# Plain float32 matmuls in place of three split float32r passes in the dense stages of a decoder layer

## The chip, the cores and the metric

The kernel runs on one core of a Trainium2 chip. The metric is the time of one execution in microseconds (us), measured on the device; lower is better.

## The reference

The reference computes one layer of a decoder trunk on 1,056 tokens (1,024 of a prompt, and 32 of eight sequences that are being decoded, four each), all in float32, with width 1,024. Cut to what matters:

```
h = rms_norm(x)
z = h @ w_in                         # u, v, q, six key/value parts, gates, merge gates
u = gelu(u); v = layer_norm(gelu(v)) # 512 wide each
o_a = u * (w_s @ v + b_s)            # causal mixing in chunks of 128 tokens
kc, vc = compress(keys), compress(values)          # dense product, gelu, dense product
o_b = g0*attend(q, kc, vc) + g1*attend(q, selected blocks) + g2*attend(q, window)
x = x + (sigmoid(g_a) * (o_a @ w_branch_a) + sigmoid(g_b) * (o_b @ w_branch_b)) @ w_out
y = x + square(relu(rms_norm(x) @ w_up)) @ w_down  # 4,096 wide
```

The caches of the decoded sequences (16 pages of 128 keys each) are compressed and attended as well.

## The kernel before

A matmul of this chip takes two forms on float32 data here. A *plain* one takes operands of type float32. One on *float32r* operands reads values that have been rounded to fewer bits of mantissa. To come near float32 accuracy with float32r, the kernel splits each operand `a` into a high part (the copy `cp` to float32r, on ScalarE) and a low part (`a - high`, on VectorE or GpSimd), and makes three passes: high times high, high times low, low times high, all adding up in one PSUM bank. Every dense product of a 128x128 stationary tile and up to 512 moving columns is three `matmul` calls.

The work in order:

- **Start and projections (0 to about 233 us).** X, scaled by the norm's gains, is kept transposed in SBUF as a high and a low tile for eight slices of 128 channels. The token-major projections (keys and values, then v, then q; `mm3`) take nine blocks of 128 tokens, each eight products of 512 columns, with weights `wt`, split ahead (`wt_split`). The feature-major parts kc, vc (`fm_k`, weights `wk`) and the gates take eight slices times three chunks of 352 tokens. The gating unit mixes v in between (`v_mix`).
- **Prompt attention (to about 741 us).** 32 pairs of 128-query block and head pair: logits, softmax, transposition of the weights P, product with the values. These matmuls are float32r already, or transposes, and aren't changed. In between run two other streams: the compression of the caches (`c_load`, `hl`), and "fillers", the dense blocks of merge gates and u that need neither attention (`fillers`, `Weights`). POOL scales P, and for those two streams it makes the low parts.
- **Attention of the decoded tokens (to about 901 us)**, which uses plain float32 matmuls before the change too: `s_acc` (logits, 512 columns; the code calls it 40 times in this stage with the ring of pages) and `values` (256 columns). The last fillers run beside it.
- **Dense tail (to the end).** Branch (16 half blocks of four slices), output projection (8 blocks of eight slices), and the MLP (64 blocks of eight slices), each slice times three chunks of 352 tokens (`fm_block`). Sources OA, OU, M, H and U are each a high and a low tile. OA and OU are read back from memory in pieces `ol` that are then split.

The weight blocks of fillers and tail come through the class `Weights`: load `wraw`, split into `whl`, one split and two loads ahead. For the fillers (`W0`) there is one buffer of each; for the tail (`W1`) two. The order of each engine's instructions is made ahead of time by the compiler's scheduler from priorities; the order of the SP queue is written by hand in the cache and page stages.

Of the kernel before, what the change touches and what calls it, by code (L numbers as in the profile page):

```python
# [45 lines left out]
def build(tc, a):  # L46
# [48 lines left out]
    class Weights:  # L95
        """The feature-major weight blocks ids, loaded and split ahead of their use."""

        def __init__(self, pl, n, ids):
            self.pl, self.n, self.ids = pl, n, list(ids)
            self.raw, self.hl, self.nl, self.ns = [], [], 0, 0  # L100
# [9 lines left out]
        def split(self):  # L110
            i = self.ids[self.ns]
            if self.nl <= self.ns:
                self.load()
            t = self.pl.tile([128, 2, 8, 128], F32R, name="whl", bufs=self.n)
            raw = self.raw.pop(0)
            with tc.high_priority():
                cp(t[:, 0], raw)
                (POOL if i < FM_BR else DVE).tensor_tensor(t[:, 1], raw, f(t[:, 0]), op=OP.subtract)  # L118
            self.hl.append(t)
            self.ns += 1  # L120

        def get(self, i):
            """Block i; its place in the order is checked."""
            if not self.hl:
                self.split()
            assert self.ids[self.ns - len(self.hl)] == i
            return self.hl.pop(0)

        def ahead(self):
            """One split and two loads past the blocks handed out."""  # L130
            used = self.ns - len(self.hl)
            while self.ns < min(used + 1, len(self.ids)):
                self.split()
            while self.nl < min(used + 2, len(self.ids)):
                self.load()
# [3 lines left out]
    ones = const("ones", [128, 128], dt=F32R)  # L139
# [8 lines left out]
    X = big.tile([128, 2, 8, NT], F32R, name="big1")  # L148
# [15 lines left out]
    DVE.memset(f(ones), 1.0)  # L164
    cp(expo, f(ones)[:, 0:16], scale=-0.5)

    # ---------------------------------------------------------------- phase 1
# [9 lines left out]
    wtr = {}  # L177

    def wt_load(g, k):
        wtr[g, k] = pr.tile([128, 512], F32, name="wtr", bufs=2)  # L180
        SP.dma_start(wtr[g, k], a["wtok"][g, k])

    def wt_split(g, k):
        t = p1.tile([128, 2, 512], F32R, name="wt", bufs=8)
        split(t[:, 0], t[:, 1], wtr.pop((g, k)))
        wt[g, k] = t

    wkr = {}

    def wk_load(i):  # L190
        wkr[i] = pw.tile([128, 8, 128], F32, name="wkr")
        SP.dma_start(wkr[i].rearrange("p k n -> p (k n)"), a["wfm"][i])

    def wk_split(i):
        t = pw.tile([128, 2, 8, 128], F32R, name="wk")
        split(t[:, 0], t[:, 1], wkr.pop(i))
        return t

    def mm3(out, xs, ws, k, first, last):
# [4 lines left out]
    def fm_k(pss, w, k, first, last, B=None):  # L204
        src = X if B is None else B
        for c in range(3):
            mm(pss[c][:, 0:TB], w[:, 0, k], src[:, 0, k, c * TB:(c + 1) * TB], first, False)
        for c in range(3):
            mm(pss[c][:, 0:TB], w[:, 0, k], src[:, 1, k, c * TB:(c + 1) * TB], False, False)
        for c in range(3):  # L210
            mm(pss[c][:, 0:TB], w[:, 1, k], src[:, 0, k, c * TB:(c + 1) * TB], False, last)
# [14 lines left out]
    wk_load(0)  # L226
# [10 lines left out]
    def x_split(k, cs):  # L237
        cp(X[:, 0, k, cs], xk[:, cs], scale=gvec[:, k:k + 1])
        DVE.scalar_tensor_tensor(X[:, 1, k, cs], xk[:, cs], gvec[:, k:k + 1], f(X[:, 0, k, cs]), op0=OP.mult, op1=OP.subtract)

    for k in range(8):
        xk = xr.pop(k)
        if k == 0:
            with tc.high_priority():
                x_split(k, slice(0, 512))
                wt_split(0, k)
                x_split(k, slice(512, NT))
            wkc = wk_split(0)
        else:
            x_split(k, slice(0, NT))  # L250
            wt_split(0, k)
# [11 lines left out]
        for n in range(NK0):  # L263
            mm3(tokps[n], slice(tok0(n), tok0(n) + 128), wt[0, k], k, k == 0, k == 7)
        fm_k(kcps, wkc, k, k == 0, k == 7)

    with tc.high_priority():
        add(accs[0], accs[0], accs[1])
        ah = [px.tile([128, NT], F32R, name="ah%d" % h, tag="xr", bufs=XRB) for h in range(2)]
        split(ah[0], ah[1], accs[0])  # L270
        pstv = pst[:, 0:18].rearrange("p (n c) -> p n c", c=2)
        for n in range(NB):
            xs = slice(tok0(n), tok0(n) + 128)
            for h in range(2):
                mm(pstv[:, n], ah[h][:, xs], ones[:, 0:2], h == 0, h == 1)
# [15 lines left out]
    wg_r = pv.tile([128, 8, 24], F32, name="wg_r")  # L291
    SP.dma_start(wg_r, a["wgate"])
    wg = pv.tile([128, 2, 8, 24], F32R, name="wg")
    for k in range(2):
# [14 lines left out]
    def head_rstd(z3, h, post):  # L309
        """z3 (128, h, 64) -> (128, h) of rsqrt(mean square + eps) * post."""  # L310
# [48 lines left out]
    def gates():  # L359
        """The attention gates, feature-major, then token-major through the tensor engine."""  # L360
        pss = [bank(*t) for t in fm3]
        for k in range(8):
            for i, j in ((0, 0), (0, 1), (1, 0)):
                for c in range(3):
                    mm(pss[c][0:24, 0:TB], wg[:, i, k], X[:, j, k, c * TB:(c + 1) * TB], k + i + j == 0, k == 7 and i == 1)
# [29 lines left out]
    def c_evac(which, pss, n0=0):  # L395
        """Raw kc / vc rows, feature-major, from their PSUM."""
# [40 lines left out]
    def comp_hidden(ps, nch, bias, pl):  # L437
        """ps (128, 2, nch): first | second halves; returns twice the gelu as (kv h, chunk)."""
# [18 lines left out]
    def comp_knorm(ps, pl, gkc, nb):  # L457
        """(chunk, (kv d)) PSUM -> normed rows in SBUF."""
# [13 lines left out]
    split(wg[:, 0], wg[:, 1], wg_r)  # L472
# [41 lines left out]
    for c in range(3):  # L514
# [7 lines left out]
        dh = pv.tile([128, 2, 384], F32R, name="dh", bufs=1)  # L522
        split(dh[:, 0, 0:w], dh[:, 1, 0:w], dg[:, 0:w])
        prb = bank("O", 1)
        for h in range(2):
            mm(prb[:, 0:w], ones, dh[:, h, 0:w], h == 0, h == 1)
        cp(rep[:, c * 384:c * 384 + w], prb[:, 0:w])
    c_evac(0, kcps)
    for n in range(NK0, NB):
        xs = slice(tok0(n), tok0(n) + 128)  # L530
        ps = bank("S", 3)
        for k in range(8):
            mm3(ps, xs, wt[0, k], k, k == 0, k == 7)
            if n == NB - 1:
                wt.pop((0, k))
                if k + 2 < 8:
                    wt_load(2, k + 2)
                wt_split(2, k)
# [4 lines left out]
    wk_load(1)  # L543
    w = wk_split(1)
# [21 lines left out]
    # the gating unit  # L566
# [12 lines left out]
    wsr = pg.tile([128, 8, 128], F32, name="wsr", tag="vh", bufs=2)  # L579
    SP.dma_start(wsr, a["wsT"])  # L580
    wsh = pg.tile([128, 2, 8, 128], F32R, name="wsh")
# [967 lines left out]
```

## Time and profile before

| | |
|---|---|
| median of three runs | 1854.61 us (1849.91 to 1858.01) |
| span of the profiled execution | 1851.7 us (nothing of its time outside the span is listed) |
| TensorE (PE) busy | 1796.6 us, 97% |
| VectorE (DVE), ScalarE (ACT), GpSimd (POOL) busy | 974.2, 718.1, 414.0 us |

PE is matmuls, PEld the loads of stationary tiles, which overlap them. A matmul's record runs from its start to its modelled end, and the next one starts before that end, so that the sum of durations, and "busy", say less than the distance from one start to the next.

### The profile page before, as it was taken

The page shows a single profiled execution, that of the slowest core. Times are in us where ns is not written, and L with a number is a line of the kernel's source. Part 1 is how long each engine was busy: PE and PEld are TensorE (multiplying, and loading weights), DVE is VectorE, ACT ScalarE, POOL GpSimd, SP SyncE. Part 2 cuts the span into 40 slices and gives each one's busy share as a digit, 9 for nine tenths or more (in the row PEclk, how much of TensorE's full clock was granted, in tenths as well). Part 3 has the DMA queues.
Part 4 walks back from the last instruction along what each step waited for, and adds up shares of the span by engine and source line. Part 5 has one row for each costly group of instructions (what it writes and reads, how often), then busy time and mean ns, then how long its engine had stood idle before and what let it go on. Part 6 is the DMA issues. An engine that isn't in the chain of part 4 may idle for free.

```text
span 1851.7 us, 30386 instructions
## 1 busy us (share of the span) xinstructions
PE 1796.6 (97%) x11031; PEld 1687.7 (91%) x11031; DVE 974.2 (53%) x2459; ACT 718.1 (39%) x1747; POOL 414.0 (22%) x604
## 2 busy tenths in 40 slices
PE   8999989999899999999899999999999999999999
PEld 6877889999899998666599999999999999999999
DVE  7637778777767777255465445333333333333332
ACT  5534577767667765233322332300330033003300
POOL 3103456555556655210000220000000000000000
PEclk9999989999999999999899999999999999999999
DMA  6232454333323314665453221111111111111121
GB/s 197 93 96 63 141 152 122 96 91 93 94 68 98 99 60 128 193 202 183 128 162 123 90 85 46 46 46 46 46 46 46 46 46 46 46 46 46 42 79 65
DMA packets 158264, 168.74 MB, mean 91 GB/s; under 512 B 52385, under 2 KB 132898, under 8 KB 158114
## 3 DMA queue, kind: packets, MB, share of 16 engines
q1 hardware_dynamic: 140466, 135.78, 23.5%
q0 software_dynamic: 6464, 20.19, 3.2%
q10 hardware_dynamic: 11184, 10.83, 1.8%
q8 instruction: 87, 1.43, 0.3%
q14 instruction: 63, 0.52, 0.1%
HBM read 136.56 MB, written 29.13 MB: 89 GB/s over the span
## 4 chain that ended last, share of the span: by engine, by line
PE 84%; DVE 6%; DMA 3%; ACT 3%; SPq 2%; issue 2%; POOL 2%; ACTq 0%; DVEq 0%; POOLq 0%
PE S L73 27%; PE G L73 17%; PE PT L73 14%; PE O L73 11%; PE F L73 11%; PE PT L844 2%; SPq L932 1%; DMA ol<-o_d 1%; ACT P L783 1%; DVE S L774 1%; DMA wraw<-wfm 1%; POOL hl L977 1%; POOL P L798 1%; DVE PH L57 1%; DMA xr<-xT 0%
## 5 line engine op out<-in xcount | busy, mean ns | idle before, releaser
L73 PE MATMUL G<-big,whl 128*128 128x352 f32 x1344 | 265.2, 338 | 2.9 <-DVE zt L57 1.5
L54 ACT ACTIVATE whl<-wraw 128x1024 fp32r<-128x1024 f32 x100 | 106.1, 1061 | 411.9 <-PE S L73 144.4
L73 PEld LDWEIGHTS G<-big,whl 128*128 128x128 f32 x1344 | 220.6, 192 | 17.6 <-issue 9.9
L73 PE MATMUL S<-U,whl 128*128 128x352 f32 x864 | 201.6, 324 | 0.0
L73 PE MATMUL S<-H,whl 128*128 128x352 f32 x840 | 190.4, 324 | 0.0
L73 PE MATMUL PT<-U,whl 128*128 128x352 f32 x576 | 154.9, 324 | 0.0
L73 PEld LDWEIGHTS S<-U,whl 128*128 128x128 f32 x864 | 150.0, 188 | 0.0
L798 POOL TENSOR_SCALAR P<-P,rs 128x128 f32<-128x128 f32 (+4 forms) x272 | 132.7, 502 | 62.3 <-DVE rs L57 40.9
L73 PEld LDWEIGHTS S<-H,whl 128*128 128x128 f32 x840 | 144.9, 188 | 0.0
L73 PE MATMUL PT<-H,whl 128*128 128x352 f32 x528 | 143.2, 324 | 0.0
L783 ACT ACTIVATE P<-S,nm 128x512 f32<-128x512 f32 (+3 forms) x208 | 108.9, 531 | 44.1 <-DVE nm L57 33.0
L73 PE MATMUL S<-wt,big 128*128 128x512 f32 x408 | 104.1, 402 | 11.4 <-ACT wt L54 7.9
L57 DVE TENSOR_TENSOR PH<-PT,PH 128x512 fp32r<-128x512 f32 (+2 forms) x160 | 98.1, 618 | 28.2 <-ACT PH L54 26.7
L118 DVE TENSOR_TENSOR whl<-wraw,whl 128x1024 fp32r<-128x1024 f32 x80 | 97.7, 1221 | 15.5 <-ACT whl L54 15.5
L73 PEld LDWEIGHTS PT<-U,whl 128*128 128x128 f32 x576 | 103.3, 188 | 0.0
L73 PEld LDWEIGHTS S<-wt,big 128*128 128x128 f32 x408 | 76.3, 191 | 28.4 <-ACT wt L54 7.9
L73 PE MATMUL F<-H,whl 128*128 128x352 f32 x312 | 101.1, 324 | 0.0
L73 PE MATMUL O<-PH,V 128*128 128x256 f32 x528 | 91.6, 295 | 8.3 <-DVE PH L57 7.9
L54 ACT ACTIVATE PH<-PT 128x512 fp32r<-128x512 f32 (+2 forms) x160 | 86.1, 544 | 34.9 <-PE PT L844 34.2
L73 PE MATMUL O<-H,whl 128*128 128x352 f32 x312 | 99.0, 324 | 0.0
L73 PE MATMUL S<-KT,QT 128*128 128x128 f32 (+3 forms) x416 | 96.2, 342 | 2.9 <-ACT P L783 2.1
L73 PE MATMUL G<-H,whl 128*128 128x352 f32 x312 | 97.5, 324 | 0.5 <-DVE r L1384 0.5
(375 smaller groups left out, 3935.5 us busy)
## 6 DMA issues: line engine op xcount, KB each, us to landing
wraw<-wfm SPq DMA_DIRECT2D x80, 512.0 KB, 3.3
ring<-cs SPq DMA_DIRECT2D x128, 128.0 KB, 2.1
wraw<-wfm POOLq DMA_DIRECT2D x20, 512.0 KB, 3.8
tg<-th_d SPq DMA_DIRECT2D x48, 176.0 KB, 2.9
qdl<-qd_d SPq DMA_DIRECT2D x64, 128.0 KB, 2.5
raw<-cck SPq DMA_DIRECT2D x128, 64.0 KB, 1.9
raw<-ccv SPq DMA_DIRECT2D x128, 64.0 KB, 1.8
wtr<-wtok SPq DMA_DIRECT2D x24, 256.0 KB, 2.6
```

Source lines behind the costliest of these rows:

```text
L54: return ACT.activation(out, in_, AF.Copy, scale=scale)
L57: return DVE.tensor_tensor(out, x, y, op=op)
L73: return PE.matmul(out, l, r, start=start, stop=stop, skip_group_check=skip)
L118: (POOL if i < FM_BR else DVE).tensor_tensor(t[:, 1], raw, f(t[:, 0]), op=OP.subtract)
L774: DVE.tensor_tensor_reduce(S, S, m, scale=-1.0, scalar=3e38, op0=OP.add, op1=OP.min, accum_out=dst)
L783: ACT.activation(Ps[c][:, lo:hi], Ss[c][:, lo:hi], AF.Exp, bias=nm[:, 0, k:k + 1], scale=todo[h, br, i], accum_out=sm[:, i, k:k + 1])
L798: POOL.tensor_scalar(P, P, rs[:, 1, k:k + 1], 1.0, op0=OP.mult, op1=OP.mult)
L844: PE.transpose(pt[:, j], Ps[c][:, j * 128:(j + 1) * 128], ident)
L932: SP.dma_start(dst, src)
L977: (POOL if qt else DVE).tensor_tensor(hl[:, 1], raw[:, :, cols], f(hl[:, 0]), op=OP.subtract)
```

## The change

All dense products, and the mixing, norm sums and cache compression, take plain float32 operands in one `matmul` call. The split tiles and their instructions go. Weights are used as loaded (`wfb`, four buffers in the tail and three for the fillers; `wt` with 16 buffers). X is one scaling on DVE. OA and OU are loaded straight into place, and M and U have two buffers.

```diff
-    X = big.tile([128, 2, 8, NT], F32R, name="big1")
+    X = big.tile([128, 8, NT], F32, name="big1")
...
     class Weights:
...
         def load(self):
-            t = self.pl.tile([128, 8, 128], F32, name="wraw", bufs=self.n)
+            t = self.pl.tile([128, 8, 128], F32, name="wfb", bufs=self.n)
...
-            t = self.pl.tile([128, 2, 8, 128], F32R, name="whl", bufs=self.n)
-                cp(t[:, 0], raw)
-                (POOL if i < FM_BR else DVE).tensor_tensor(t[:, 1], raw, f(t[:, 0]), op=OP.subtract)
...
         def ahead(self):
-            while self.ns < min(used + 1, len(self.ids)):
-                self.split()
-            while self.nl < min(used + 2, len(self.ids)):
+            while self.nl < len(self.ids) and len(self.raw) < self.n - 1:
                 self.load()
...
-        mm(out, X[:, 0, k, xs], ws[:, 0], first, False)
-        mm(out, X[:, 0, k, xs], ws[:, 1], False, False)
-        mm(out, X[:, 1, k, xs], ws[:, 0], False, last)
...
+            DVE.tensor_scalar(X[:, k, cs], xk[:, cs], gvec[:, k:k + 1], None, op0=OP.mult)
...
-            mm3(ps, xs, wt[0, k], k, k == 0, k == 7)
+            mm(ps, X[:, k, xs], wt[0, k], k == 0, k == 7)
...
-            for qt in range(4):
-                hl = pa.tile([128, 2, 16, 32], F32R, name="hl", bufs=HIB)
-                    cp(hl[:, 0], raw[:, :, cols])
-                    (POOL if qt else DVE).tensor_tensor(hl[:, 1], raw[:, :, cols], f(hl[:, 0]), op=OP.subtract)
...
-                    mm(out, w1[:, 0, qt * 2 + o], hv[:, o], qt + o == 0, False)
-                    mm(out, w1[:, 1, qt * 2 + o], hv[:, o], False, False)
-                    mm(out, w1[:, 0, qt * 2 + o], lv[:, o], False, qt == 3 and o == 1)
+            rv = raw.rearrange("p g (o k r) -> p o k g r", k=2, r=8)
+            for o in range(8):
+                mm(out, w1[:, o], rv[:, o], o == 0, o == 7)
...
-    W1 = Weights(wst, 2, range(FM_MG + NF0, N_FM))
+    W1 = Weights(wst, 4, range(FM_MG + NF0, N_FM))
...
-    W0 = Weights(wst0, 1, range(FM_MG, FM_MG + NF0))
+    W0 = Weights(wst0, 3, range(FM_MG, FM_MG + NF0))
...
-                t = olp.tile([128, TB], F32, name="ol", bufs=OLB)
-                ACT.dma_start(t[:, 0:e], o_d[4 * half + k, :, cs])
-                split(dst[:, 0, k, cs], dst[:, 1, k, cs], t[:, 0:e])
+            e = NP if half else NT
+            ACT.dma_start(dst[:, k, 0:e], o_d[4 * half + k, :, 0:e])
...
     def fm_block(w, src, ks, woff=0):
...
             for c in range(3):
-                mm(pss[c][:, 0:TB], w[:, 0, k + woff], src[:, 0, k, c * TB:(c + 1) * TB], first, False)
-            for c in range(3):
-                mm(pss[c][:, 0:TB], w[:, 0, k + woff], src[:, 1, k, c * TB:(c + 1) * TB], False, False)
-            for c in range(3):
-                mm(pss[c][:, 0:TB], w[:, 1, k + woff], src[:, 0, k, c * TB:(c + 1) * TB], False, last)
+                mm(pss[c][:, 0:TB], w[:, k + woff], src[:, k, c * TB:(c + 1) * TB], i == 0, i == len(ks) - 1)
...
-                DVE.scalar_tensor_tensor(r, pss[c][:, 0:TB], 0.0, r, op0=OP.max, op1=OP.mult)
-                cp(U[:, 0, fo, cs], r)
-                sub(U[:, 1, fo, cs], r, f(U[:, 0, fo, cs]))
+                DVE.scalar_tensor_tensor(U[:, fo, cs], pss[c][:, 0:TB], 0.0, r, op0=OP.max, op1=OP.mult)
```

## Rows read from the trace of the kernel before

**Rows 1.** The page: busy time of the engines, and PE in 40 equal slices.
```profile
PE 1796.6 (97%) x11031; PEld 1687.7 (91%) x11031; DVE 974.2 (53%) x2459; ACT 718.1 (39%) x1747; POOL 414.0 (22%) x604
...
PE   8999989999899999999899999999999999999999
```
**Rows 2.** Four stretches: length, busy time (instructions) by engine, granted clock, DMA share, GB/s.
```profile
0.00:233.00 233.00, 221.37 (x1144) 185.64 (x1145) 155.95 (x394) 112.69 (x215) 65.47 (x69) 1.00 0.37 117
233.00:741.00 508.00, 478.93 (x3396) 461.09 (x3394) 381.05 (x1213) 348.39 (x1014) 302.15 (x485) 0.98 0.34 100
741.00:901.00 160.00, 153.18 (x728) 101.83 (x728) 67.27 (x207) 51.08 (x150) 23.45 (x30) 0.99 0.58 180
901.00:1852.00 951.00, 943.08 (x5766) 939.18 (x5766) 369.96 (x648) 205.93 (x370) 22.94 (x21) 0.99 0.19 65
```
**Rows 3.** The chain that ended last: start us, us, what, and how many instructions.
```profile
130.25 11.42 PE S L73 x48
...
254.84 2.38 POOL whl L118
...
1263.57 11.68 PE S L73 x72
```
**Rows 4.** The stretches after 233 us, instructions on `whl` alone (columns as in Rows 2).
```profile
233.00:741.00 508.00, 211.50 (x1104) 180.97 (x1104) 0.00 (x0) 17.97 (x17) 38.94 (x17) 0.98 0.34 100
741.00:901.00 160.00, 73.88 (x337) 55.28 (x337) 2.45 (x2) 5.28 (x5) 9.39 (x4) 0.99 0.58 180
901.00:1852.00 951.00, 942.75 (x5760) 938.32 (x5760) 95.26 (x78) 82.81 (x78) 0.00 (x0) 0.99 0.19 65
```
**Rows 5.** PE groups: line, engine, operation, out<-in, shape, count, busy us, mean ns, idle before.
```profile
L73 PE MATMUL S<-wt,big 128*128 128x512 f32 x408 | 104.1, 402 | 11.4 <-ACT wt L54 7.9 <-ACT vz L54 3.1 <-DVE wt L57 0.3
...
L844 PE MATMUL PT<-ident,P 128*128 128x128 f32 x560 | 90.1, 278 | 6.0 <-DVE QT L57 3.4 <-DVE PH L57 1.2 <-POOL P L798 1.2
...
L73 PE MATMUL F<-hl,w1s 128*128 128x256 f32 x384 | 62.0, 286 | 0.0
...
L73 PE MATMUL S<-ring,qp 128*128 128x512 f32 x80 | 43.3, 625 | 2.6 <-DMA ring<-cs 2.2 <-DMA ring<-cw 0.4
...
L73 PE MATMUL G<-wt,big 128*128 128x512 f32 x144 | 40.4, 405 | 0.0
...
L73 PE MATMUL F<-wt,big 128*128 128x512 f32 x96 | 24.9, 395 | 0.0
```
**Rows 6.** PE's weight loads in order of time, 791 to 794 us.
```profile
791.63 0.19 PEld L73 LDWEIGHTS S<-ring,qp 128*128 128x128 f32 x1 [0.24 <-issue]
792.06 0.19 PEld L73 LDWEIGHTS S<-ring,qp 128*128 128x128 f32 x1 [0.24 <-issue]
792.49 0.19 PEld L73 LDWEIGHTS G<-big,whl 128*128 128x128 f32 x1 [0.24 <-issue]
```
**Rows 7.** The chain between 780 and 800 us.
```profile
783.06 1.87 PE O L73 x8
...
794.04 0.86 PE S L73 x2
```
**Rows 8.** PE in order of time, 572 to 580 us.
```profile
576.50 1.59 PE L73 MATMUL F<-hl,w1s 128*128 128x256 f32 x12
```
**Rows 9.** The chain's shares in 0 to 233, 233 to 741 and 901 to 1852 us.
```profile
by line: PE S L73 34.4%; PE F L73 14.2%; PE G L73 13.5%; PE PT L73 12.9%; DMA xr<-xT 3.7%; issue 2.5%; DVE big L239 2.0%; DVE acc L258 2.0%; DVE wt L57 1.5%; PE O L352 1.5%; DVE vs L57 1.5%; PE O L73 1.4%; DVE vy L595 1.1%; POOL vst L161 0.
...
by line: PE G L73 27.2%; PE S L73 10.0%; PE O L73 8.8%; PE PT L844 8.1%; PE F L73 7.1%; issue 3.6%; ACT P L783 3.0%; DVE S L774 2.4%; DMA wraw<-wfm 2.1%; POOL hl L977 2.0%; POOL P L798 2.0%; DVE PH L57 1.9%; ACT PH L54 1.6%; PE PT L699 1.4%
...
by line: PE S L73 36.1%; PE PT L73 23.4%; PE G L73 12.6%; PE O L73 12.5%; PE F L73 12.5%; DMA ol<-o_d 1.6%; DVE oa L57 0.3%; issue 0.1%; ACT ou L54 0.1%; ACT oa L54 0.1%; DVE ot L1199 0.1%; DVE ou L57 0.1%; DVE r L1384 0.1%; DVE t L57 0.1%;
```
**Rows 10.** POOL's groups in 233 to 741 us: count, busy us, mean ns, idle before.
```profile
L977 POOL TENSOR_TENSOR hl<-raw,hl 128x512 fp32r<-128x512 f32 x48 | 61.4, 1288 | 39.4 <-ACT hl L54 31.5 <-DMA raw<-cck 7.5 <-POOL o_o L873 0.3
...
L118 POOL TENSOR_TENSOR whl<-wraw,whl 128x1024 fp32r<-128x1024 f32 x17 | 41.2, 2426 | 18.7 <-ACT whl L54 17.5 <-POOL o_o L873 1.2
```

More of the change, by code (lines that the diff above doesn't have):

```diff
@@ L138, in build @@
     ident = const("ident", [128, 128])
-    ones = const("ones", [128, 128], dt=F32R)
+    ones = const("ones", [128, 128])
     rep = const("rep", [128, NT])
@@ L163, in build @@
     POOL.memset(onesf, 1.0)
-    DVE.memset(f(ones), 1.0)
-    cp(expo, f(ones)[:, 0:16], scale=-0.5)
+    DVE.memset(ones, 1.0)
+    cp(expo, ones[:, 0:16], scale=-0.5)
     pq = pool("pq")
@@ L268, in build @@
         add(accs[0], accs[0], accs[1])
-        ah = [px.tile([128, NT], F32R, name="ah%d" % h, tag="xr", bufs=XRB) for h in range(2)]
-        split(ah[0], ah[1], accs[0])
         pstv = pst[:, 0:18].rearrange("p (n c) -> p n c", c=2)
         for n in range(NB):
-            xs = slice(tok0(n), tok0(n) + 128)
-            for h in range(2):
-                mm(pstv[:, n], ah[h][:, xs], ones[:, 0:2], h == 0, h == 1)
+            mm(pstv[:, n], accs[0][:, tok0(n):tok0(n) + 128], ones[:, 0:2], True, True)
         ms = px.tile([128, NB], F32, name="ms")
@@ L290, in build @@
     SP.dma_start(gq, a["gq"])
[L291 to L294, printed above, removed]
+    wg = pv.tile([128, 8, 24], F32, name="wg")
+    SP.dma_start(wg, a["wgate"])
+    for k in range(8):
         wt_load(2, k)
@@ L521, in build @@
             DVE.tensor_scalar(dg[:, 256:288], ident[:, 96:128], rtok[:, 8:9], None, op0=OP.mult)
-        dh = pv.tile([128, 2, 384], F32R, name="dh", bufs=1)
-        split(dh[:, 0, 0:w], dh[:, 1, 0:w], dg[:, 0:w])
         prb = bank("O", 1)
-        for h in range(2):
-            mm(prb[:, 0:w], ones, dh[:, h, 0:w], h == 0, h == 1)
+        mm(prb[:, 0:w], ones, dg[:, 0:w], True, True)
         cp(rep[:, c * 384:c * 384 + w], prb[:, 0:w])
@@ L542, in build @@
         evac_next()
-    wk_load(1)
-    w = wk_split(1)
+    for k in range(8):
+        wt.pop((0, k))
+    w = wk_load(1)
     vcps = [bank(*t) for t in fm3]
@@ L951, in c_weights @@
     def c_weights(which):
-        w1r = pa.tile([128, 8, 128], F32, name="w1r", tag="hl", bufs=HIB)
-        ACT.dma_start(w1r, a["w1" + "kv"[which]])
-        w1 = pa.tile([128, 2, 8, 128], F32R, name="w1s", bufs=1)
-        split(w1[:, 0], w1[:, 1], w1r)
+        w1 = pa.tile([128, 8, 128], F32, name="w1s", bufs=2)
+        ACT.dma_start(w1, a["w1" + "kv"[which]])
         pe = small([128, 8, 2], "pes", 1, p=pa)
@@ L1362, in stats2 @@
             cs = slice(c * TB, (c + 1) * TB)
-            ah2 = [p4.tile([128, TB], F32R, name="ah2", tag="sq5", bufs=2) for _ in range(2)]
-            split(ah2[0], ah2[1], acc2[:, cs])
             ps = dbank()
-            mm(ps[:, 0:TB], ones, ah2[0], True, False)
-            mm(ps[:, 0:TB], ones, ah2[1], False, True)
+            mm(ps[:, 0:TB], ones, acc2[:, cs], True, True)
             DVE.tensor_scalar(R2[:, cs], ps[:, 0:TB], 1.0 / 1024, EPS, op0=OP.mult, op1=OP.add)
```

145 lines of the change are left out of this document (36 added, 109 removed).

## The prediction, on record before the changed kernel was run

> **What bounds the kernel now.** I read the page first: PE is busy for 97% of the span, and in nearly every slice [rows 1]. Since a matmul's record overlaps the next one's, that share doesn't say how full PE is, so the next view was the stretches [rows 2], and then the chain that ended last [rows 3], where each matmul counts only for what it adds. In the tail the reader is to see blocks of 72 passes of 352 columns in 11.68 us, 0.1622 us each, and 5,760 such passes in the last 951 us [rows 4]: 934 of 951 us at that distance. The tail is bound by PE alone; off PE the chain there has little more than the reading of OA and OU (`ol`, 1.6%, 15 us) [rows 9]. The first 233 us are nearly as full once the first X has come. In the prompt attention the chain is on PE for only some 63% of 508 us in the shares listed [rows 9]; the rest is the softmax on ACT, DVE and POOL. PE is kept going there by the fillers, but the chain can't be shortened by PE alone.
>
> **What a product costs before and after.** Before, three passes: 352 columns 3 x 0.1622 = 0.487 us. At 512 columns, 48 passes took 11.42 us on the chain [rows 3], 0.238 each; the 352-column price scaled by columns gives 0.236. I take that: 0.708 us for three. At 256 columns, 12 in 1.59 us, less the last one's record of 0.286, is 11 distances of 0.119 [rows 8, 5]: 0.356 us for three.
>
> After, no row shows a plain product of 352 columns with a 128x128 stationary tile. The nearest is the 512-column logit of the decoded tokens. The code calls it 40 times and the trace has 80 matmuls [rows 5]: a plain product is two instructions, each with its own weight load. The loads of one run start at 791.63, 792.06 and 792.49 us [rows 6], and the chain gives 0.86 us to two [rows 7]: 0.43 us per instruction, 0.86 per product. Per column that is 0.00168 us a product, against 3 x 0.000461 = 0.00138 for three float32r passes. So the change takes one call for three but 1.22 times the time of PE. For 352 columns 0.86 x 352/512 = 0.591 us (+0.105 over 0.487), for 256 0.430 (+0.074), for 512 0.86 (+0.152). A weight load takes 0.19 us [rows 6] and lies under an instruction of 0.296 us, so I cost it at nothing; if it weren't hidden, it would show as more.
>
> From below the bound is the same rate (no row shows a plain product cheaper per column; the 256-column ones with a 64-wide tile add 0.234 us an instruction on the chain [rows 7], more than 0.215). From above: each of two instructions costs twice a float32r pass of the same columns, 2 x 2 x 0.1622 = 0.649 us. I take 0.591, because the 512-column row is at the same stationary size.
>
> A page speaks against the change and prices it differently. The row is the two instructions 0.43 us apart [rows 6]. The Trainium skill, "FP8 and Floating Point Precision", section TensorE Precision Notes, says that true FP32 takes four passes through the array. By that rule with the float32r pass as the pass, a product would be 0.649 us and the tail alone 311 us longer; with the rate of the row it is 0.591 and 202. The trace agrees with a factor of that size (0.86 to 0.236 us, 3.6), and the row decides on the rate.
>
> The other end is in the Trainium skill too: "TensorE: Matmul & The Clock Gate", section Back-to-back issue gap, puts a warm matmul at N/2.4 + 2.5 ns, an estimate of 0.149 us for 352 columns. By it three passes would be 0.447 us and the change would cost 0.145 a product, 278 us in the tail. The tail's 72 in 11.68 us [rows 3] differ from it (0.162), so the sum goes by the row.
>
> **The change part by part.**
> - *Tail*: 5,760/3 = 1,920 products [rows 4], each +0.105: **+202 us**, on the path, with nothing to hide it.
> - *Fillers*: (1,104 + 337)/3 = 480 products [rows 4] at +0.105: **+50**.
> - *Projections*: 648 passes of 512 columns [rows 5], 216 products at +0.152: **+33**. kc, vc and gates are 72 products of 352 by the code's loops: **+8**. v's mixing, 32 of 256 columns: **+2**.
> - *Cache compression*: 384/3 = 128 products [rows 5] at +0.074: **+9**.
> - The norm sums and the broadcast of norms are under 20 small products: +2, left out.
>
> Work of PE added: 304 us, of which 202 + 43 stand in stretches where PE sets the pace and 59 in the attention.
>
> What it removes: the splits. In the tail they hide (95 us of DVE and 83 of ACT on `whl` against 951 [rows 4]), so nothing is gained there but the `ol` pieces: a whole slice lands in place by one transfer, where pieces landed in four buffers, were split and made room for the next, so of their 15 us on the chain, between none and all, I take back **10**; the ACT queue has 8 transfers to issue for 24. At the start, `wt` on DVE (1.5% of 233, 3.5 us [rows 9]) goes, and X is one pass: **5**. In the attention POOL loses 61 us of `hl` and 41 of `whl`, and waits in front of them of 39 and 19 [rows 10]; P's scaling stands behind these in POOL's order, and PE's transposes wait for P. On the chain `hl` has 2.0% of 508 us, 10 us, and the first `whl` 2.4 [rows 9, 3]. `W0` has three buffers for one, so a filler block needn't wait for the split of its weights. I take the 12 on the chain and about as much again for P that comes sooner (its scaling has another 2.0%): **22**. The rest of the attention's chain isn't on PE, so a part of the 59 us that are added there can fill idle time of PE, between none and all of it; since the order is fixed beforehand and the fillers run on past 741 us already [rows 4], I take a fifth: **12**. Moves cost nothing I can see: loads of weights go out on the same queues, and have a block of 14 us to come in.
>
> Queues: the raw pages are freed now by the last of eight products, not by the split, and SP's order is fixed, so the loads behind them (`qdl`) may come later; eight products are 3.4 us, and two buffers cover that. If not, it is a few us over 16 batches, in the range.
>
> Sum: 1851.7 + 304 - 49 = 2107 us of span. The median of the runs is 2.9 us above the span, so about **2110 us**, 13.8% slower.
>
> **The rivals.**
> 1. *Nothing is given back* in the attention and elsewhere: 1851.7 + 304 + 3 = 2159. For it: the order is fixed beforehand and PE is already busy in every slice. Against it: the waits of POOL [rows 10].
> 2. *The attention takes all it is given*: of 508 us it isn't PE that the chain needs, so fillers and compression fit into idle time (-59 for -12): 304 - 96 = +208, 2063. For it: the chain's shares. Against it: the fillers run on into the stretch after 741 us already, so more of them can only be later.
> 3. *The pass is priced as float32r's*: 0.649 a product, +0.162. 2,472 products of 352 give +400, 216 of 512 (2 x 2 x 0.236 - 0.708) +51, 160 of 256 +19: 470 - 49 = 2276. Against it the 0.43 us.
> 4. *Faster*: a plain product is one instruction, as the plain transposes are (560 in the trace [rows 5], one for each call by the code's loops). At 0.296 us a product of 352 columns would be 0.191 cheaper, 470 us for 2,472, and the time near 1380. It decides below 0.487 us a product. Against it the 80 matmuls for 40 calls.
>
> **How the numbers follow.** The forecast (2090 to 2130) has 0.45, rival 1 (2130 to 2175) 0.20, rival 2 (2050 to 2090) 0.25, rival 3 0.06, rival 4 0.01, other 0.03. The range from 2062 to 2165 takes the forecast and the centres of rivals 1 and 2, and leaves out 0.2. The forecast's own range is 2090 to 2130. Under 0.5% (9 us) a change of this kernel can't be told from none. All but rival 4 and a part of the other are slower by over 0.5%: faster 0.01, same 0.01, slower 0.98.
>
> **What would show it.** In the profile after: PE with 2/3 of the instructions for dense work; a block of the tail as 48 matmuls in 14.2 us, their starts 0.296 us apart (15.6 for rival 3); the tail beginning at about 964 us instead of 901, and some 192 us longer; no `hl` or `whl` on POOL, and P's scaling with less waiting. The forecast is wrong if the distance isn't 0.296 us, or if the stretch up to the tail grows by less than 20 or more than 105 us.

## The result, and the profile after

The changed kernel takes 2173.8 us (2169.8 to 2176.0) where the kernel before takes 1852.3 (median of four runs): a ratio of 1.173, with a 95% interval of 1.1707 to 1.1762. It is slower, as forecast, but by 322 us where 258 were forecast: 64 us above the forecast of 2110, and 9 above the upper end of the range. The profiled execution took 2169.8 us, its span 2168.0.

The page of the kernel after, PE's rows: busy time, share, instructions, and the 40 slices (they answer to [rows 1]).
```profile
PE 2105.4 (97%) x8179; PEld 1384.9 (64%) x8179; DVE 729.7 (34%) x2157; ACT 506.7 (23%) x1405; POOL 283.4 (13%) x527
...
PE   8999989999999987998999999999999999999999
```
PE has 2,852 instructions fewer and 309 us more of busy time; DVE, ACT and POOL have lost 245, 211 and 131 us. They were not what the time hung on.

Four stretches of the kernel after, cut at the same events as [rows 2]: the end of the projections, the end of the prompt attention, the first matmul of the branch, the end. Columns as there.
```profile
0.00:270.00 270.00, 263.53 (x785) 134.80 (x786) 123.78 (x327) 75.67 (x138) 49.25 (x51) 0.99 0.29 99
270.00:843.00 573.00, 549.84 (x2969) 436.49 (x2967) 334.60 (x1207) 305.41 (x941) 201.60 (x427) 0.98 0.30 87
843.00:1024.00 181.00, 152.25 (x582) 82.08 (x580) 73.50 (x233) 47.17 (x158) 13.31 (x28) 0.94 0.59 185
1024.00:2168.00 1144.00, 1139.73 (x3846) 731.51 (x3846) 197.78 (x390) 78.41 (x168) 19.22 (x21) 1.00 0.15 51
```
Against [rows 2] the projections grow from 233 to 270 us (+37; forecast 43 less 5), the tail from 951 to 1,144 (+193; forecast +192). What lies between them grows from 668 to 754 (+86), and there the forecast had +25: 59 of work less 34 given back. So nearly all of the miss, 61 us, sits in the two middle stretches.

The tail's blocks on the chain of the kernel after, the answer to the 11.68 us for 72 passes of [rows 3].
```profile
1239.15 14.20 PE S L73 x48
1340.32 14.20 PE S L73 x48
```
14.20/48 is 0.296 us an instruction, 0.592 a product; the forecast took 0.591 from the 512-column logit.

PE's groups of the kernel after (columns as in Rows 5). The count of `wt` is 2/3 of [rows 5], as is that of the cache products: two instructions for three passes.
```profile
L73 PE MATMUL S<-wt,big 128*128 128x512 f32 x272 | 125.0, 609 | 6.5 <-DMA wt<-wtok 6.5
L73 PE MATMUL F<-raw,w1s 128*128 128x256 f32 x256 | 61.3, 381 | 0.0
L767 PE MATMUL PT<-ident,P 128*128 128x128 f32 x560 | 87.8, 275 | 3.2 <-DVE PH L57 1.9 <-DVE nm L57 0.7 <-DVE rs L717 0.4
```

Now the stretch that missed. The chain's shares in 300 to 700 us, the middle of the prompt attention, in the kernel before:
```profile
by line: PE G L73 28.3%; PE S L73 11.1%; PE O L73 9.9%; PE PT L844 9.2%; PE F L73 7.9%; ACT P L783 2.8%; issue 2.5%; POOL hl L977 2.5%; DVE S L774 2.5%; POOL P L798 2.2%; DVE PH L57 1.8%; SPq L932 1.7%; DMA raw<-ccv 1.7%; PE PT L699 1.5%; D
```
and in the kernel after:
```profile
by line: PE G L73 49.0%; PE F L73 15.3%; PE S L73 12.8%; PE O L73 10.8%; PE PT L767 9.4%; PE PT L622 2.5%; PE F L903 0.2%
```
Before, some 68% of these 400 us are PE, and the rest the softmax and the splits. After, it is PE for all of it, so that nothing that makes PE's work longer is hidden there. POOL lost its splits (`hl`, `whl` of [rows 10]), but P's scaling doesn't wait less. POOL's group of P in the attention, before:
```profile
L798 POOL TENSOR_SCALAR P<-P,rs 128x128 f32<-128x128 f32 (+4 forms) x262 | 129.2, 507 | 59.6 <-DVE rs L57 38.6 <-ACT PH L54 7.9 <-ACT P L783 6.5
```
and after:
```profile
L721 POOL TENSOR_SCALAR P<-P,rs 128x128 f32<-128x128 f32 (+4 forms) x272 | 127.7, 486 | 150.5 <-DVE rs L57 109.3 <-ACT P L706 21.3 <-PE O L73 11.4
```
POOL has less to do now and stands idle for `rs`, the softmax's sums. That these come later because the logits come later from PE fits the chain above, but isn't shown by itself.

The fillers also lie otherwise. PE's instructions on `wfb` in the two middle stretches, the answer to the 1,104 and 337 of [rows 4]:
```profile
270.00:843.00 573.00, 258.45 (x816) 152.14 (x816) 10.05 (x17) 0.98 0.30 87
843.00:1024.00 181.00, 47.18 (x144) 27.58 (x144) 1.65 (x3) 0.94 0.59 185
```
Before, 77% of the fillers' passes ran in the prompt attention; after, 85% of their instructions do, and the last of these starts at 764 us, 79 us ahead of the attention's end. The stretch behind it has less to fill PE with.

One thing more differs. The issue of the transfer for `kct`, the compressed keys that the decoded tokens' attention begins with, before:
```profile
L1050 SPq DMA_DIRECT2D kct<-c_d x1: 371/371/371, 700.0 to 700.0; - x1
```
and after:
```profile
L961 SPq DMA_DIRECT2D kct<-c_d x1: 371/371/371, 846.6 to 846.6; - x1
```
Before, it goes out 37 us ahead of the attention's end (737), and the first logit of the ring starts at 751, 14 us behind that end. After, it goes out 4 us behind the end (843), and the ring's first logit starts at 878, 35 us behind. A prelude of some 21 us that lay under the attention has come out from under it.

### The profile page after: what moved, and what is told of

It is laid out like the page before. It is cut to its first block, busy times and chain, and to the rows that moved or that the text cites. A ratio compares the mean times of both kernels' runs of the same rounds, so it can differ in the third digit from the quotient of the medians.

```text
span 2168.0 us, 23876 instructions
## 1 busy us (share of the span) xinstructions
PE 2105.4 (97%) x8179; PEld 1384.9 (64%) x8179; DVE 729.7 (34%) x2157; ACT 506.7 (23%) x1405; POOL 283.4 (13%) x527
## 4 chain that ended last, share of the span: by engine, by line
PE 81%; DMA 2%; DVE 2%; SPq 1%; issue 1%; ACT 1%; POOL 0%; ACTq 0%; DVEq 0%; POOLq 0%
PE S L73 24%; PE G L73 19%; PE PT L73 13%; PE F L73 11%; PE O L73 11%; PE PT L767 2%; SPq L855 1%; PE PT L622 1%; DVE PH L57 1%; DMA ring<-cw 0%; DMA ou<-o_d 0%; ACT P L706 0%; DMA ring<-cs 0%; DMA pes<-pek 0%; DVE S L697 0%
## 5 line engine op out<-in xcount | busy, mean ns | idle before, releaser
L73 PE MATMUL G<-big,wfb 128*128 128x352 f32 x896 | 285.8, 465 | 5.0 <-DMA wfb<-wfm 4.8
L73 PEld LDWEIGHTS G<-big,wfb 128*128 128x128 f32 x896 | 167.7, 192 | 86.5 <-DMA wfb<-wfm 5.0
L73 PE MATMUL S<-U,wfb 128*128 128x352 f32 x576 | 190.6, 459 | 0.0
L73 PE MATMUL S<-H,wfb 128*128 128x352 f32 x560 | 184.5, 459 | 0.0
L73 PEld LDWEIGHTS S<-U,wfb 128*128 128x128 f32 x576 | 109.4, 190 | 61.0
L73 PEld LDWEIGHTS S<-H,wfb 128*128 128x128 f32 x560 | 106.4, 190 | 59.3
L73 PE MATMUL PT<-U,wfb 128*128 128x352 f32 x384 | 133.8, 459 | 0.0
L73 PE MATMUL PT<-H,wfb 128*128 128x352 f32 x352 | 123.1, 459 | 0.0
L767 PE MATMUL PT<-ident,P 128*128 128x128 f32 x560 | 87.8, 275 | 3.2 <-DVE PH L57 1.9
L697 DVE CUSTOM_DVE_ANT_0 S<-S,mask 128x256 f32<-128x256 f32 (+3 forms) x160 | 75.6, 484 | 21.2 <-PE S L73 18.1
```

The costliest lines, as they stand in the source:

```text
L73: return PE.matmul(out, l, r, start=start, stop=stop, skip_group_check=skip)
L697: DVE.tensor_tensor_reduce(S, S, m, scale=-1.0, scalar=3e38, op0=OP.add, op1=OP.min, accum_out=dst)
L767: PE.transpose(pt[:, j], Ps[c][:, j * 128:(j + 1) * 128], ident)
```

## The experiments

Two theories stood at the start. *Placement*: without `hl` the compression's pool `pa` is 8 KB per partition smaller, the pools behind it slide down over buffers of the attention, and the prelude must wait for those to come free. *Price*: the attention gives nothing back, since PE is now its bound. Rivals for the second came with the runs: fewer buffers, fillers too early, pieces too long. Letters in an expectation are those that it defines. Where products are left out or made twice it is said.

For the stretch from projections to branch I use one measure throughout: its length less PE's work, the sum over its matmuls of the usual start-to-start distance of their shape (352 columns: 0.160 us float32r, 0.296 plain; 256: 0.116 and 0.216; a transpose 0.108). An estimate, since a few records are missing, but the same for all; time at a lower granted clock (0.94 in 843 to 1,024 us above, 0.99 before) counts as idle in it. Before: 668 us, 570 of work, 98 idle. After: 754, 638, 116.

**Pools as before (`pad`).**
```diff
-        w1 = pa.tile([128, 8, 128], F32, name="w1s", bufs=2)
+        w1 = pa.tile([128, 8, 128], F32, name="w1s", bufs=4)
```


> The changed kernel with 8 KB per partition more in the pool of the cache compression (w1s with four buffers for two), so that the pools of the decoded tokens' attention lie where they lay in the kernel before; same work. Theory A (place in memory): in the changed kernel the prelude of the decoded tokens' attention (q_pad, kct) can't start before the last pair of the prompt attention has let go of its tiles, 846 us; with the padding it starts under the attention again, the gap of 35 us from the attention's last product to the first logit of the ring shrinks to about 14 as before, and the time falls by 15 to 30 us, to 2145 to 2160. Theory B (PE's work alone sets the pace up to the tail): the prelude moves but the time stays within 5 us of 2174.

Measured: 2152.6 us (2152.0 to 2153.2), ratio 1.162 [1.1593, 1.1649]: 21 us less than the kernel after, for two buffers that hold nothing new. The `kct` transfer of `pad`:
```profile
L961 SPq DMA_DIRECT2D kct<-c_d x1: 367/367/367, 648.0 to 648.0; - x1
```
It is under the attention again, and the ring's first logit starts 15 us behind the attention's end. Idle 100 instead of 116. Placement held, and is worth 21 of the 64 us. The runs from here on stand on `pad`, or on the kernel before.

**The tail alone (`tail`)**: the head of the kernel before, and of the change only the part from the branch on.
```diff
-    W1 = Weights(wst, 2, range(FM_MG + NF0, N_FM))
+    W1 = Weights(wst, 1, range(FM_MG + NF0, FM_BR))
+    W2 = Plain(wst, 3, range(FM_BR, N_FM))
...
-    M = mp.tile([128, 2, 8, NT], F32R, name="M", tag="big2")
+    M = mp.tile([128, 8, NT], F32, name="M", tag="big2", bufs=2)
```


> The kernel before up to the tail, and the changed tail (branch, output projection and MLP on plain operands, OA and OU loaded straight): one part of the change alone. Theory A (the tail's price is 1,920 products at 0.105 us, less the 10 us of the pieces that were read and split): the part from the first branch matmul to the end takes 1144 us as in the changed kernel instead of 951, and the time is 2035 to 2055 us. Theory B (a part of the tail's price comes from the head's late fillers and DMAs): under 2025.

Measured, one execution: 2048.9 us, +198 over 1851.3. Its windows:
```profile
0.00:904.00 904.00, 851.76 (x5266) 747.14 (x5267) 606.52 (x1818) 511.45 (x1374) 393.15 (x583) 0.99 0.40 122
904.00:2047.00 1143.00, 1139.06 (x3846) 731.06 (x3845) 198.18 (x390) 78.67 (x168) 19.21 (x21) 1.00 0.16 51
```
The head is that of before but for 3 us, the tail that of after but for 1. The term of the tail stands by itself.

**The compression alone (`comp`)**: the kernel before with plain products for the cache only, and its pool kept at its size.
```diff
-            for qt in range(4):
-                hl = pa.tile([128, 2, 16, 32], F32R, name="hl", bufs=HIB)
...
+            rv = raw.rearrange("p g (o k r) -> p o k g r", k=2, r=8)
+            for o in range(8):
+                mm(out, w1[:, o], rv[:, o], o == 0, o == 7)
```


> The kernel before with one part of the change alone: the cache compression on plain operands, without its 64 copies on ACT and 64 subtractions on POOL and DVE (61 us of POOL in the attention). 128 products at 0.074 us more are 9 us of PE. Theory A (the forecast's: POOL's splits stand in the way of the scaling of P, and their going gives back 10 us of the chain and some 5 more): 0 to 10 us faster. Theory B (POOL's work has cover, PE's doesn't): 3 to 10 us slower.

Measured: 1852.8 us against 1850.8, ratio 1.0010 [0.9999, 1.0021]. 11 us of work more (256 x 0.216 for 384 x 0.116), 2 us of time, between the ranges of the two theories: the going of the cache's splits gives back about 9 us, where theory A has some 15.

**The splits again, for nobody (`dum`)**: `pad` with the cache's splits into `hl` made again and not read.
```diff
+            for qt in range(4):
+                hl = pa.tile([128, 2, 16, 32], F32R, name="hl", bufs=HIB)
+                cols = slice(qt * 32, (qt + 1) * 32)
+                with tc.high_priority():
+                    cp(hl[:, 0], raw[:, :, cols])
+                    (POOL if qt else DVE).tensor_tensor(hl[:, 1], raw[:, :, cols], f(hl[:, 0]), op=OP.subtract)
```


> The padded kernel, but ACT, POOL and DVE make the splits of the raw cache pages again, which nothing reads (the tile takes the place of the padding). Theory A (the forecast's: their going is worth some 15 us in the attention): 10 to 25 us over the padded kernel's 2152.6. Theory B (they have cover): within 5 us of it.

Measured: 2176.2 us, ratio 1.1754 [1.1727, 1.1782], 24 us above `pad`. The chain of `dum` in 300 to 700 us:
```profile
by line: PE G L73 16.8%; SPq L855 14.3%; PE F L73 10.4%; issue 7.6%; DMA raw<-ccv 5.3%; PE S L73 4.4%; DMA raw<-cck 4.2%; PE O L73 3.8%; ACT P L706 3.7%; ACT hl L54 3.6%; PE PT L767 3.6%; DMA qsl<-qd_d 2.0%; DVE PH L57 2.0%; DVE S L697 1.9%
```
The splits hold the raw pages, so their loads stand on the chain beside POOL's work: the run bounds what the splits could cost (24), and doesn't price POOL alone. With `comp`, 9 to 24.

**One buffer for the fillers' weights (`one`)**: `pad` with `W0` at one buffer, its place kept.
```diff
-    W0 = Weights(wst0, 3, range(FM_MG, FM_MG + NF0))
+    W0 = Weights(wst0, 1, range(FM_MG, FM_MG + NF0))
+    wpad = wst0.tile([128, 2, 8, 128], F32, name="wpad", bufs=1)
```


> As the padded kernel, but the fillers' weights have one buffer again for three (its place in the pool is kept by a tile that nothing uses). Theory A2 (three buffers let the fillers run ahead of the prompt attention, which then ends without any): the fillers come later, under 14 of 17 blocks by the 28th pair instead of 17, the attention is shorter by 15 to 40 us, fillers are left for the decoded tokens' attention, and the time is 10 to 30 us under the padded kernel's. Theory B (PE's work alone): each block now waits for its weights, some 4 us a block of which other work covers a part; the time is the padded kernel's or up to 20 us more.

Measured: 2152.7 us, ratio 1.1621 [1.159, 1.1652], that of `pad`. The three buffers neither helped, as the prediction had it, nor let the fillers run ahead to any harm.

**Filler work taken out and put in (`fill1`, `fill12`)**: `pad` with one of eight products in each filler chunk (seven eighths of the merge gates' and u's products are left out), and with twelve (four of them made twice).
```diff
-                for k in range(8):
-                    mm(ps[:, 0:TB], w[:, k], X[:, k, cs], k == 0, k == 7)
+                for k in range(12):
+                    mm(ps[:, 0:TB], w[:, k % 8], X[:, k % 8, cs], k == 0, k == 11)
```


> As the padded kernel, but each filler chunk makes one of its eight products (7/8 of the merge gates' and u's products are left out; weight loads and evacuations stay): 420 products less, 249 us of PE. Theory A (PE is shared, and the fillers' matmuls set the attention's pace): the prompt attention, 561 us in the changed kernel, falls to 350 to 420 us. Theory B (the forecast's: the attention's chain runs mostly off PE, so that PE work fits into idle time): it stays above 480 us.

> The padded kernel with 12 products in each filler chunk instead of 8 (four are made twice, so that merge gates and u come out otherwise): 240 products more, 142 us of PE. Theory A (with plain products PE alone is the chain of the attention): 130 to 150 us over 2152.6. Theory B (still 0.7 us for the us, as on the way from an eighth of the products to all): 90 to 110 over it.

Measured, one execution each: 1975.9 and 2256.1 us, -177 for -249 us of work and +103 for +142, 0.71 and 0.73 a microsecond (theory B of `fill12`). The attention of `fill1` takes 417 us, within theory A's range. The chain of `fill1` in 300 to 700 us is mixed again:
```profile
by line: PE F L73 15.2%; PE S L73 10.0%; PE O L73 9.9%; PE PT L767 7.3%; DVE PH L57 6.8%; DMA th_d<-zt 5.5%; issue 5.3%; ACT P L706 4.9%; DVE S L697 4.8%; PE G L73 3.6%; ACT PH L54 2.4%; DVE nm L695 2.0%; DMA qsl<-qd_d 1.5%; DMA qdl<-qd_d 1
```
A filler costs neither all nor nothing. The prediction's "a fifth fits into idle time" is near the 0.28 of these two runs, but they change the number of the fillers' products, and not the length of one.

**The fillers alone (`fillp`)**: the kernel before, with the 17 filler blocks of `W0` plain, in three buffers (the low part of X is left out of their products).
```diff
+                    if W is W0:
+                        mm(ps[:, 0:TB], w[:, k], f(X[:, 0, k, cs]), k == 0, k == 7)
+                        continue
...
-    W0 = Weights(wst0, 1, range(FM_MG, FM_MG + NF0))
+    W0 = Plain(wst0, 3, range(FM_MG, FM_MG + NF0))
```


> The kernel before with the 17 filler blocks of the attention on plain operands, raw weights in three buffers (the low part of X is left out of these blocks' products). 408 products at 0.105 us are 43 us of PE more; 17 splits of weights go (41 us of POOL, 18 of ACT). Theory A (the forecast's: a fifth of PE's work falls into idle time, and the splits' going gives back as much again): 15 to 30 us slower, 1866 to 1882. Theory B (PE's work is paid for at 0.7 us in the us, as the kernel with an eighth of the fillers' products has it, with nothing back for the splits): 28 to 35 slower. Theory C (paid in full): 40 to 50 slower.

Measured: 1903.2 us against 1850.8, ratio 1.0278 [1.0258, 1.0298]: +52 us for 17 x 24 products, 43 us of work, although their splits are gone. The chain of `fillp` in 300 to 700 us:
```profile
by line: PE G L73 49.6%; PE S L73 13.0%; PE O L73 11.4%; PE PT L871 9.9%; PE F L73 9.7%; PE PT L726 2.0%; SPq L959 0.6%; DVE nm L57 0.6%; issue 0.6%; POOL hl L1004 0.5%; DMA raw<-cck 0.5%; DVE S L801 0.4%; ACT P L810 0.2%; PE F L1017 0.2%; 
```
That is above all three theories. The plain fillers alone turn the attention's chain into PE, and cost more than their work. Between the attention's matmuls, fillers come in runs of 1.25 us in the mean before and 2.26 in `fillp` (2.31 in `pad`), 300 to 700 us.

**Fillers moved or spread (`nf14`, `nf11`, `spread`)**: `pad` with 14 or 11 filler blocks in the attention for 17, the rest behind it; and with the loads of the blocks tied to the attention's progress.
```diff
-NF0, NF1 = 17, 0
+NF0, NF1 = 14, 0
```


> The padded kernel with 14 of the 17 filler blocks in the stream that may run in the prompt attention; three more go to the other stream, whose weights' place is free only after it. Same work. Theory A (the fillers crowd the attention and are then missing beside the decoded tokens' attention): the prompt attention is some 30 us shorter (3 blocks of 14.2 us at 0.7), the stage behind it, with 41 us of idle PE, some 15 to 25 longer; the time falls by 5 to 20 us, to 2133 to 2148. Theory B (the sum of PE's work sets the head, wherever it lies): within 5 us of 2152.6.

> The padded kernel with 11 of the 17 filler blocks in the stream that may run in the prompt attention. Theory A: six blocks of 14.2 us leave the attention (some 60 us shorter) and more than fill the idle time of the stage behind it (45 to 60 longer, since 85 us of work meet 41 idle); the time is 0 to 20 us under 2152.6. Theory B: within 5 us of 2152.6.

> The padded kernel, where the load of filler block b waits until a given pair of the prompt attention is done (a one-element copy on POOL per pair and per block carries the order), so that the blocks are spread over the attention as in the kernel before (9 of 17 by the 28th pair instead of 15); same work for PE. Theory A (the removed splits do free the attention, but the fillers use that up by running ahead, and idle time of PE is left at the attention's end): the time falls by 10 to 40 us, to 2113 to 2143. Theory B (the idle time of PE, some 125 us between projections and tail, comes with the softmax chain wherever the fillers lie): 2147 to 2165.

Measured: 2152.7 us, 1.1621 [1.1591, 1.1652]; 2158.0, 1.1653 [1.1625, 1.1681]; 2157.3, 1.1653 [1.1629, 1.1677], against 2152.6. With 11 blocks the attention is 63 us shorter (505 for 568) and what stands behind it 68 longer (233 for 164). Idle 97, 106 and 103, for 100. So to move whole blocks, or to hold back their loads, only moves the idle time: in `nf11` the attention's fillers are used up at 622 us, 160 us ahead of its end, and in `spread` they last to 787 us of 794, but with ten gaps of 8 to 23 us between them.

**Shorter pieces (`half`)**: `pad` with each filler product of 352 columns as two of 176, the same columns and the same weights.
```diff
-                    mm(ps[:, 0:TB], w[:, k], X[:, k, cs], k == 0, k == 7)
+                    for h in range(2):
+                        hs = slice(c * TB + 176 * h, c * TB + 176 * h + 176)
+                        mm(ps[:, 176 * h:176 * h + 176], w[:, k], X[:, k, hs], k == 0 and h == 0, k == 7, True)
```


> The padded kernel with each of the fillers' products made in two halves of 176 columns: the same columns for PE, so that 480 products are 960 of half the length and the attention's matmuls can go between pieces of 0.296 us, as they could go between passes of 0.162 us in the kernel before, and not between pieces of 0.592. Theory A (a matmul of the attention that has become ready waits for the filler's product in hand, and that costs the 21 us by which the plain fillers in the kernel before cost more than 0.72 of their work): 8 to 20 us under the padded kernel's 2152.6. Theory B (the length of a piece is nothing): within 5 us of it, or up to 5 over it for the starts of 960 more instructions.

Measured: 2117.5 us (2116.7 to 2118.0), ratio 1.1432 [1.1407, 1.1456], 35 us under `pad` where theory A had 8 to 20, with 480 products more for PE to begin and the same columns. A stretch of `pad`, PE in order of time:
```profile
471.70 0.72 PE L73 MATMUL O<-PH,V 128*128 128x256 f32 x4
472.26 3.71 PE L73 MATMUL G<-big,wfb 128*128 128x352 f32 x12
475.54 0.66 PE L73 MATMUL S<-KT,QT 128*128 128x512 f32 x1
```
and the same place of the attention in `half`:
```profile
443.05 0.72 PE L73 MATMUL O<-PH,V 128*128 128x256 f32 x4
443.61 2.55 PE L73 MATMUL G<-big,wfb 128*128 128x176 f32 x16
445.88 0.51 PE L73 MATMUL S<-KT,QT 128*128 128x512 f32 x1
```
and the chain of `half` in 300 to 700 us:
```profile
by line: PE G L73 32.6%; PE F L73 15.9%; PE S L73 14.8%; PE O L73 12.6%; PE PT L767 11.2%; PE PT L622 2.6%; SPq L855 1.3%; issue 1.2%; DVE rkA L57 1.0%; DVE PH L57 1.0%; DVE S L697 0.9%; DVE rkB L57 0.9%; DMA raw<-cck 0.4%; ACT P L706 0.3%;
```
The run of fillers in front of the next logit is 3.3 us long in the one and 2.3 in the other; over 300 to 700 us the runs of `half` last 1.21 us in the mean, and other engines are back on the chain. Idle falls from 100 to 60 us. Where that idle time was, the attention and the stage behind it show, in `pad`:
```profile
274.00:842.00 568.00, 548.13 (x2976) 436.03 (x2976) 337.70 (x1201) 301.27 (x933) 202.63 (x424) 0.99 0.31 89
842.00:1006.00 164.00, 144.49 (x537) 74.94 (x535) 59.18 (x199) 42.47 (x136) 11.19 (x21) 0.97 0.61 192
```
and in `half`:
```profile
279.00:773.00 494.00, 485.93 (x3395) 470.16 (x3394) 326.42 (x1175) 290.31 (x917) 193.75 (x406) 0.98 0.33 95
773.00:974.00 201.00, 199.64 (x1076) 150.22 (x1075) 68.25 (x218) 48.92 (x150) 20.31 (x38) 1.00 0.54 171
```
PE has no record running for 20 and 20 us in `pad`, for 8 and 1 in `half`. In `pad` it isn't in the middle of the attention, where PE is the whole chain, but at its end. The chain of `pad` in 740 to 842 us:
```profile
by line: PE G L73 21.8%; issue 10.2%; DVE PH L57 10.1%; PE S L73 10.1%; PE O L73 10.0%; PE PT L767 8.4%; DVE S L697 6.6%; ACT P L706 5.1%; DVE nm L695 3.0%; POOL P L721 2.9%; DVE QT L57 1.8%; DVE nm L57 1.3%; DVE nm L697 1.3%; ACT PH L54 1.
```
All fillers of the attention's 17 blocks are used up there at 771 us, 71 us ahead of its end. In `half` the attention is 73 us shorter, so 390 of these blocks' 1,632 pieces are still left at its end, and the stage behind it, 37 us longer, is full with them. In PE's order a run holds about as many instructions whatever their length: in the mean of 300 to 700 us 6.7 before, 8.2 in `pad`, 8.3 in `half` and `fillp`. So shorter pieces make shorter runs, and the attention gets further on each microsecond of fillers.

**Shorter pieces elsewhere (`fillph`, `half2`, `bhalf`)**: `fillp` with its plain filler products in halves; `half` with the cache products of 256 columns in halves too; and the kernel before with its float32r filler passes in halves.
```diff
+                        o = ps[:, 176 * h:176 * h + 176]
+                        mm(o, w[:, 0, k], X[:, 0, k, hs], k == 0 and h == 0, False, True)
+                        mm(o, w[:, 0, k], X[:, 1, k, hs], False, False, True)
+                        mm(o, w[:, 1, k], X[:, 0, k, hs], False, k == 7, True)
```


> The kernel before with its 17 filler blocks of the attention on plain operands (the low part of X left out of them), as in the run that was 52 us slower for 43 us of PE, now with each product in two halves of 176 columns. Theory A (pieces of 0.592 us were what cost more than the work): 25 to 38 us over the kernel before (0.72 x 43 = 31), 1876 to 1889. Theory B (halves help only in the padded kernel, by another order): 45 or more over it, above 1896.

> The padded kernel with halved fillers, and the cache compression's products of 256 columns also in two halves of 128. Theory A (length of the piece, whoever's it is): 128 products of 0.43 us become pieces of 0.22; by their number against the fillers' 480 products of 0.59 (35 us), 3 to 8 us under 2117.5. Theory B (only the fillers, which have the lowest priority, stand in the way): within 3 us of it.

> The kernel before with each float32r pass of the fillers in two halves of 176 columns. Theory A (length of the piece): 0.162 us is short already, and at 176 columns a pass is 0.081 us against a weight load of 0.19 us beside it, so that it may be held up by the loads: between 5 us faster and 40 us slower. Theory B (any cut gives the attention room): 10 or more us faster, under 1841, and so faster than both kernels.

Measured: `fillph` 1856.2 us against 1853.3, ratio 1.0018 [1.0006, 1.0030]: +3 us where `fillp` had +52, better than expected. `half2` 2115.0, 1.1419 [1.1399, 1.1438], 2.5 us under `half`, within theory B's 3. `bhalf` 2049.4, 1.1068 [1.1004, 1.1132]: 196 us slower, far more than expected, and with its own cause. Its windows behind the attention:
```profile
691.00:874.00 183.00, 171.94 (x956) 118.68 (x955) 62.03 (x196) 48.69 (x151) 21.20 (x23) 0.93 0.50 150
874.00:1112.00 238.00, 219.64 (x1005) 215.54 (x1005) 34.92 (x64) 24.66 (x46) 30.42 (x40) 0.50 0.13 43
```
and a block of fillers in its attention, on the chain:
```profile
310.08 3.62 PE G L73 x31
```
At full clock a half pass takes 0.117 us there (3.62/31), not half of 0.162, so splitting float32r passes adds work: 2,880 x (0.117 - 0.081) is some 104 us. And the last thousand of them, with no other matmul beside them, ran at a granted clock of 0.50, 1.2 GHz, for 238 us, 0.213 us from start to start for 0.111 to 0.117 at 2.4 GHz. The attention is shorter, 457 us for 503, but fewer fillers run in it: 1,339 of 2,880 half passes, where before it was 1,082 of 1,440 passes.

None of these beats the kernel before; the nearest that leaves nothing out is `comp`.

## Why the prediction was wrong

**What held.** The direction, the bound of the tail, and the unit: two instructions a product, 0.592 us for 0.591. The tail, +193 for +192, is shown alone by `tail` (+198). The projections, +37 for +38. Rival 3 (0.649 a product) would have shown blocks of 15.6 us; they are 14.20. Rival 4 needed one instruction a product. The forecast's own test spoke: the stretch up to the tail grew by 123 us (901 to 1,024), over the 105 that it named.

The Trainium skill, "TensorE: Matmul & The Clock Gate", section Back-to-back issue gap, was set aside in the prediction, since float32r passes came 0.162 us apart and its N/2.4 + 2.5 ns gives 0.149. (By it the change would cost 0.144 a product and 276 us in the tail, for the prediction's 0.145 and 278.) For the plain instruction, read as 704 columns, which is an assumption, it gives an estimate of 0.296, and the trace agrees (14.20/48). It was right for the added operation and low for the removed one.

**The step that failed** is the 34 us that the sum gives back between projections and branch: the **22** for the splits that go and for P that comes sooner, and the **12** for a fifth of 59 us that was to fit into idle time of PE. Measured there: +86 us. Work is 65 to 68 of it by the distances (fillers +54, compression +11; the forecast had 59), and idle time didn't fall but grew from 98 to 116. None of the 34 came back. Rival 1, nothing given back (2159), was nearer, and still too low; that its range (2130 to 2175) holds the time is in part luck, since 21 us of it have a cause that the rival doesn't name. In place of that step the runs showed:

1. *A price that the sum didn't have: the placement of pools*, 21 us (`pad`). The prediction costed moves at nothing and never asked what a smaller tile does to the addresses of the pools behind it.
2. *The give-back exists, but the longer piece takes it away*, 35 us (`half`). In `half`, with runs of fillers as long as before's (1.21 for 1.25 us), idle is 60 us, 38 under before; the forecast had 34. In `pad` it is 100, as before. The prediction priced a plain product by its work alone, and held that a softer bound elsewhere would absorb some. But a plain instruction holds PE 0.296 us where a pass held it 0.162, and runs of fillers between the attention's matmuls, of about as many instructions, grew from 1.25 to 2.3 us. The attention's chain goes matmul, softmax on three engines, matmul, and its next matmul comes behind such a run. So the fillers are used up before the attention ends, and from there on PE waits for the softmax. `fillp` and `fillph` repeat it on the kernel before: +52 us with long pieces, +3 with short, for the same 43 us of work.
3. *Work under-sized*, some 6 us: 65 for 59.

21 + 35 + 6 are 62 of the 64 us; the first two are differences of runs, the third an estimate, so that they add up so closely is in part luck. With the first two undone, `half` takes 2117.5, inside the range and 7.5 above the forecast.

**What fell.** That the fillers' buffers matter (`one`); that it helps to move whole blocks of fillers or to hold them back (`nf14`, `nf11`, `spread`), though it is true that they are used up too early; that P's scaling waits less once POOL has lost its splits: POOL is idle 91 us longer in front of P than before.

**What stays open.** Why the scheduler's order has runs of about as many instructions, whatever the length of one: the traces show it, and not the reason. Whether the 40 us that `fillph` gives back come from the splits' going or from runs still shorter (1.02 us) than before's: both changed there. What the cache's splits cost apart from the pages that they hold: 9 to 24 us with them. Why the clock of `bhalf` stayed at half.

## What to carry to other kernels

Work that is slipped in beside a chain of short dependent steps is priced twice: by its time on the engine, and by how much of it stands in front of the chain's next step; with runs of about as many pieces, to halve the plain products of 352 columns, at nearly no cost in work, gave 35 us here. See too where the filling work runs out: from there on the chain's idle time has no cover. A forecast of what comes back when an engine is relieved needs the chain of the kernel after, not of before: where PE had become the whole chain, nothing of POOL's relief was seen. And where a tile changes its size, see which pools move with it, and which later load then waits for an earlier stage's buffers.

## What the runs showed of the hardware

- A plain float32 product is two instructions, 0.296 us apart at 352 columns and 0.149 at 176 (26 on the chain of `half` in 3.88 us): half the columns, half the time. A float32r pass is 0.162 at 352 and 0.111 to 0.117 at 176, so halving it saves little. Passes of 128 and of 64 columns in the attention of the kernel before come 0.11 us apart too (medians within runs of one shape), so columns don't set that distance. Each has its own load of a 128-column tile, which is the likely floor; no run here took it away.
- The granted clock fell to 1.2 GHz in `bhalf` when only short float32r passes were left to PE, after it had been at 0.93 in the stretch before, and stayed there up to the tail. The tail's passes of 352 columns, alone on PE as well, ran at 0.99 before [rows 2].

The piece in the chain of `half`:
```profile
363.28 3.88 PE G L73 x26
```
